# An attention block with a gated feed-forward part on one Trainium2 core: pools of the output projection and of the feed-forward part laid at two ends of SBUF, and the first three feed-forward weights split beside the last row blocks of the projection

## Chip, cores and metric

The kernel runs on one core of one Trainium2 chip. The metric is the device time of one execution in microseconds (us). A change of 0.2% (5.65 us) is about what a measurement of this kernel can tell from no change.

## The reference

One layer of a pre-normalised residual block, for an input x of 2048 rows by 1024 columns in float32. Cut to what matters:

```
u = rms_norm(h, norm1_w);  p = u @ w_in
y_A = differential attention (4 heads);  y_B = stick-breaking attention (8 heads)
h = h + concat(y_A, y_B) @ w_out
u2 = rms_norm(h, norm2_w)
h = h + (silu(u2 @ w_gate) * (u2 @ w_up)) @ w_down      # w_gate, w_up: 1024 x 2816; w_down: 2816 x 1024
```

## The kernel before

Every float32 operand is split into two float16 parts (a rounded value `hi` and a rest `lo`, under a power-of-two scale), and each product is three float16 matmuls. The order of the instructions on each engine is fixed beforehand by a scheduler that follows the text, priorities and its own timeline; each engine and the DMA queue of SyncE (SP) then works its list strictly in order. Nearly all transfers are issued on SP's queue.

**First part.** Eight groups of heads are projected and attended (`proj`, `diff_attn`, `sb_attn`). While the last group is attended, `out_proj` (line 744) begins: for each of 16 row blocks t it loads the mixed heads (`mt`) and the block of x (`xf`), makes four sums of 24 matmuls of 128x128 by 128x256 in two PSUM banks (tag `pj`, line 758), adds them into `xf` on VectorE (DVE, line 761) and writes `xf` to the DRAM tensor `hd`. For t below 12, `post` (line 773) also normalises the block and `x_ops` (line 226) forms from each pair of blocks seven operands for Strassen-like products, written to `xcd[0]` (rows 0 to 1023) and `xcd[1]` (rows 1024 to 2047). Row blocks 12 to 15 are normalised later, by `build_x`.

**Second part.** The feed-forward width of 2816 is cut into 11 pieces (fg) of 256, and the rows into two halves of 1024: 22 steps. A step has a gate `quad` and an up `quad`, each of seven products of 12 matmuls of 128x128 by 128x512 (line 917) on the seven operands X of the half and one split weight (`wg`, `wu`); after every second step `down` (line 1007, its matmuls in line 1014) follows with `wd` on the two steps' activations. So the first `down` of the kernel stands after the gate products of step 2.

In the first half each weight piece is prepared by `load_ffn` (line 833): a 1 MB load into `fst` (two buffers, line 815), squares on ScalarE (`sq`, line 850) or the maximum (line 185), sums over rows on TensorE (`fsc`, line 858 for wg and wu, line 178 for wd), a short chain of small DVE operations for the scale, then `hi` (lines 211, 213, 215), `lo` (line 216, DVE) and the sums of blocks (line 99). The result, 1.8 MB, is also written to the DRAM tensor `split`, from which the second half reads it. The `fst` buffer is free for the next load when its weight is split, so on SP's list a `split` write and the next `fst` load stand one behind the other, as a pair of 2.8 MB.

`build_x` (line 1063) runs during steps 0 and 1: it loads blocks 12 to 15 from `hd` (`bx`), normalises them and forms their operands. It does so in eight rounds: split into float16 (`b`), a DMA transposition of `b` into one buffer (line 236), and a write of that buffer to `xcd[1]` (line 237). The buffer is single, so a round's transposition waits for the write of the round before. The tile `b16` that holds all this is one of the two buffers of the tag `act`; the activations of step 0 take the other one, and those of step 1 (line 976) wait until the last write has read `b16`.

All of the first part's pools are closed, and the second part's opened over them: the first instruction of the new pools waits until the old ones are done with. The loads of X and of the first weights are held to an order with the `mt` loads by hand (`XO`, `WO`, `after_mt`).

Of the kernel before, what the change touches and what calls it, by code (L numbers as in the profile page):

```python
# [39 lines left out]
XO = (10, 13, 14, 15, 11, 12, 15)  # L40
WO = (10, 14, 15)
# [19 lines left out]
def block(tc, a, out):  # L61
# [3 lines left out]
    with top:  # L65
# [44 lines left out]
        def nm(s):  # L110
            uid[0] += 1
            return f"{s}{uid[0]}"
# [138 lines left out]

        with ExitStack() as ph1:
            sp = ph1.enter_context(tc.tile_pool(name="sp", bufs=2))
            bias = sp.tile([P, 4, 256], F32, name="bias", bufs=1)
            ps = ph1.enter_context(tc.tile_pool(name="ps", bufs=2, space=PSUM))
            zp = ph1.enter_context(tc.tile_pool(name="zp", bufs=1))
            pjs = ExitStack()
            pp = pjs.enter_context(tc.tile_pool(name="pp", bufs=2))
# [22 lines left out]
            def load_w(g, st=None):  # L281
# [6 lines left out]
                pt = ps.tile([P, 512], F32, tag="pj", name=nm("wsc"))  # L288
# [26 lines left out]
            @pri("pm")  # L315
            def proj_tile(G, xt):
                pj = ps.tile([P, 512], F32, tag="pj", name=nm("pj"))
# [81 lines left out]
            @pri("spl")  # L399
            def split_t(src, n, he="ADP", le="DP"):  # L400
                s16 = sp.tile([P, 2048], F16, tag="s16", bufs=SB, name=nm("s16"))
# [286 lines left out]
            mpt = ps.tile([P, 512], F32, tag="pj", name=nm("msc"))  # L688
# [30 lines left out]
            wos, kos, mts, rp2 = [], [], [], []  # L719

            def load_wo(n):
                if n in (0, 3):
                    t16 = pp.tile([P, 2 * KT * 384], F16, tag="w16", bufs=2, name=nm("wo"))
                    hi, lo = t16[:, :2048], t16[:, 2048:4096]
                elif n == 1:
                    t16 = pp.tile([P, KT, 384], F32, tag="wst", bufs=1, name=nm("wo"))[:].rearrange("p k n -> p (k n)").bitcast(F16)
                    hi, lo = t16[:, :2048], t16[:, 2048:4096]
                else:
                    hi, lo = (pp.tile([P, 4, 256], F32, tag="raw", name=nm("wo"))[:].rearrange("p t n -> p (t n)").bitcast(F16) for _ in range(2))
# [4 lines left out]
                sW = weight_scale([st[:, :D] for st in sts], rW[:], pW[:], ps.tile([P, 512], F32, tag="pj", name=nm("osc")), hi[:, :D].bitcast(mybir.dt.bfloat16))  # L734
# [9 lines left out]
            def out_proj():  # L744
                for t in range(NT):
# [3 lines left out]
                    xf = pp.tile([P, 6, 4, 2, 64], F16, tag="st", name=nm("xf"))[:].rearrange("p c t s e -> p (c t s e)").bitcast(F32)[:, :D]  # L749
                    SP.dma_start(xf, x[t * P : (t + 1) * P, :])  # L750
                    for h in range(2):
                        po = ps.tile([P, 512], F32, tag="pj", name=nm("po"))
# [19 lines left out]
            @pri("ox")  # L772
            def post(t, xf):
                if t % 2 == 0:
                    held[:] = [z4(), z4()]
                xn = held[t % 2]
                norm_tile(xf, xn[:, :D], w2)
                for h in range(2):
                    ACT.copy(xn[:, 512 * h : 512 * h + 512], transposed(xn, 512 * h)[:])
                note("D", 1150)  # L780
                note("A", 1000)
                if t % 2 == 1:
                    for _ in x_ops([z[:, :D].rearrange("p (d n) -> p d n", d=2) for z in held], z4()[:, :D].rearrange("p (d n) -> p d n", d=2), t // 8, t % 8 // 2, lambda: (sp.tile([P, 2048], F16, tag="s16", bufs=SB, name=nm("x16"))[:], None)):
                        pass
# [11 lines left out]
            for _ in op:  # L796
                pass
            pjs.close()

        with ExitStack() as ph2:  # L800
            ps2 = ph2.enter_context(tc.tile_pool(name="ps2", bufs=2, space=PSUM))
            fw = ph2.enter_context(tc.tile_pool(name="fw", bufs=2))
            xops = []
            for o in range(7):
                xp = ph2.enter_context(tc.tile_pool(name=f"xp{o}", bufs=1))
                xops.append(xp)
            fp = ph2.enter_context(tc.tile_pool(name="fp", bufs=2))
            hp = ph2.enter_context(tc.tile_pool(name="hp", bufs=1))
            r_2, p_2, r_24 = rp2
            scales = {}  # L810

            def after_mt(d, k):
                tc.add_manual_dep(d.ins, mts[k].ins.name, mybir.DependencyInfo(mybir.DependencyClass.NoSync, mybir.DependencyReason.DATA), reason="issue order")

            def stage(fg, nme):
# [6 lines left out]
                if fg == 0:  # L822
                    after_mt(d, WO["gud".index(nme)])
                return st

            ones = hp.tile([P, P], BF16, name="ones", bufs=1)
# [6 lines left out]
            def load_ffn(half, fg, names, W):  # L833
                eng = "ADP" if fg == 0 else WE
                sc = scales.setdefault(fg, {})
                for nme in names:
                    if half == 1:
                        yield
                        late = nme == "d" and fg == NFG - 1
                        w16 = fw.tile([P, 7, 2, 512], F16, tag="wd" if nme == "d" and not late else "wgu", bufs=2, name=nm("w" + nme))  # L840
# [12 lines left out]
                    w16 = fw.tile([P, 7, 2, 512], F16, tag="wd" if nme == "d" else "wgu", bufs=2, name=nm("w" + nme))  # L853
                    pt = ps2.tile([P, 512], F32, tag="b", bufs=8, name=nm("fsc"))
# [65 lines left out]
            def quad(wv, X, tag, bufs, c11, hook=None):  # L920
                def pst(t):
                    return ps2.tile([P, 512], F32, tag="b", bufs=8, name=nm(t))

# [83 lines left out]
            def down(half, units, hs, last, hook=None):  # L1007
# [8 lines left out]
                def pst():  # L1016
                    return ps2.tile([P, 512], F32, tag="b", bufs=8, name=nm("pd"))

# [6 lines left out]
                for j in range(4):  # L1025
# [9 lines left out]
                    pa = pst()  # L1035
# [3 lines left out]
                    pb = pst()  # L1039
                    prod(pb, 4, 4, j)  # L1040
                    acc(u2[:], pb, u2[:])
                    pc = pst()
# [4 lines left out]
                    pd = pst()  # L1047
# [5 lines left out]
                    pe = pst()  # L1053
# [29 lines left out]

            ticks = build_x()
# [5 lines left out]
            level()  # L1090
            steps = [(h, f) for h in range(2) for f in range(NFG)]
            units = []
            W = {}
            X = None
            hs = None
            for i, (half, fg) in enumerate(steps):
                if fg == 0:
                    if half == 0:
                        load_now(0, 0, "g", W)
                    X = [None] * 7  # L1100
                    for o in (0, 4, 5, 1, 2, 6, 3):
                        X[o] = xops[o].tile([P, 4, 2, 4, P], F16, tag=f"X{o}", name=nm("X"))
                        d = SP.dma_start(X[o][:].rearrange("p t s k n -> p (t s k n)"), xcd[half][o].rearrange("p t n -> p (t n)"))
                        if half == 0:
                            after_mt(d, XO[o])
                    if half == 0:
                        load_now(0, 0, "u", W)
# [22 lines left out]
                def in_down():  # L1130
                    end("g")
                    begin("d", half, fg, "d", W)
# [47 lines left out]
```

## Time and profile before

| | |
|---|---|
| median of 3 runs | 2825.47 us (2822.91 to 2825.56) |
| the profiled execution, its time | 2822.35 us |
| its span, first to last instruction | 2820.6 us |
| TensorE busy / VectorE / ScalarE / GpSimd | 89% / 71% / 48% / 52% |
| mean granted TensorE clock | 0.957 |
| bytes moved by DMA | 555.57 MB, mean 197 GB/s |

A profile names instructions by engine (PE: TensorE matmuls, PEld its weight loads, DVE, ACT, POOL, SPq: issues on SP's queue), line, operation and tiles (out<-in). In a timeline a row is its start, its length, what it is and, in brackets, how long the engine had been idle before it and what it had waited for. In the table by stretches a number with (x) is an engine's busy time with its count of instructions; behind them stand the granted clock, the DMA engines' busy share and GB/s. DMA rows give the size and the median time from issue to landing.

### The profile page before, as it was taken

The numbers are of one execution on the slowest core, as the hardware profiler recorded it, in microseconds if no ns is written. First come the engines' busy times: TensorE is split into PE (matmuls) and PEld (weight loads), VectorE is DVE, ScalarE is ACT, GpSimd is POOL, SyncE is SP. The second block draws the span as 40 slices with busy tenths as digits, with TensorE's granted clock in tenths as the row PEclk, the third lists the DMA queues.
The fourth block names the chain that finished last, engine by engine and source line by source line (L and its number), as shares of the span: only waits on it lengthen the run. The fifth ranks groups of instructions, "written<-read, shape, count | busy, mean of one in ns | idle before, by whom it ended". The sixth has DMA issues, their size and how long they took to land.

```text
span 2820.6 us, 45459 instructions
## 1 busy us (share of the span) xinstructions
PE 2505.3 (89%) x17052; PEld 1410.6 (50%) x17052; DVE 2003.0 (71%) x3780; ACT 1358.3 (48%) x2534; POOL 1452.7 (52%) x1011
## 2 busy tenths in 40 slices
PE   7998888988888776789887798989989999999997
PEld 4565555555555443467773344444444444444443
DVE  6898879787989999876729677777785643434435
ACT  4665656467777888655615434444342212111111
POOL 3567767664545545546626456556564332322323
PEclk9999999999999798999998899999999999999998
DMA  7788888789999898987978855656656744645634
GB/s 235 193 164 177 161 175 169 175 173 202 216 196 203 158 189 150 194 182 198 217 257 272 256 193 181 220 198 211 217 203 250 302 164 165 224 143 186 219 128 164
DMA packets 663724, 555.57 MB, mean 197 GB/s; under 512 B 521216, under 2 KB 588800, under 8 KB 653264
## 3 DMA queue, kind: packets, MB, share of 16 engines
q1 hardware_dynamic: 661680, 550.59, 72.0%
q8 instruction: 133, 2.18, 0.3%
q0 software_dynamic: 512, 1.36, 0.2%
q10 hardware_dynamic: 1312, 0.72, 0.1%
q14 instruction: 87, 0.71, 0.1%
HBM read 265.27 MB, written 151.52 MB: 148 GB/s over the span
## 4 chain that ended last, share of the span: by engine, by line
PE 36%; DVE 11%; DMA 9%; issue 5%; POOL 4%; ACT 4%; SPq 1%; DVEq 0%; POOLq 0%; ACTq 0%
PE pd L1014 14%; PE pm L917 8%; PE pa L917 6%; PE pd L917 5%; DVE z L559 4%; DMA aT<-s 2%; POOL s L99 2%; DVE wd L216 1%; DMA fst<-in_w_up_dram 1%; DMA fst<-in_w_down_dram 1%; PE po L758 1%; DVE z L560 1%; PE pj L322 1%; DMA xcd<-b 1%; DMA b<-b 1%
## 5 line engine op out<-in xcount | busy, mean ns | idle before, releaser
L99 POOL TENSOR_TENSOR s<-z,s 128x1024 f16<-128x1024 f32 (+7 forms) x288 | 474.7, 1657 | 330.9 <-ACT s L90 301.1
L322 PE MATMUL pj<-w,xt 128*128 128x384 f16 x3072 | 571.6, 334 | 25.4 <-DMA xt<-xs 9.0
L1014 PE MATMUL pd<-wd,act 128*128 128x512 f16 x1848 | 412.4, 383 | 16.3 <-ACT act L976 8.7
L322 PEld LDWEIGHTS <-xt 128*128 128x128 f16 x3072 | 300.3, 100 | 235.1 <-issue 37.5
L450 PE MATMUL sc<-kT,qT 128*128 128x512 f16 (+3 forms) x1280 | 347.0, 361 | 76.1 <-DVE z L560 27.6
L559 DVE TENSOR_TENSOR_SCAN z<-z,sc 128x512 f32<-128x512 f32 (+3 forms) x320 | 355.4, 1113 | 74.0 <-ACT sc L557 71.3
L460 PE MATMUL yp<-v,aT 128*128 128x64 f16 (+1 forms) x4896 | 282.1, 208 | 78.3 <-DMA aT<-s 77.7
L460 PEld LDWEIGHTS <-aT 128*128 128x128 f16 x4896 | 245.3, 102 | 169.4 <-DMA aT<-s 107.0
L99 POOL TENSOR_TENSOR act<-cg,act 128x512 f16<-128x512 f32 x118 | 165.3, 1410 | 284.7 <-ACT act L976 284.7
L99 POOL TENSOR_TENSOR hs<-hs,cu 128x512 f32<-128x512 f32 x138 | 178.5, 1301 | 249.4 <-DVE cu L1023 103.3
L917 PEld LDWEIGHTS <-wg 128*128 128x128 f16 x1848 | 184.9, 100 | 243.6 <-issue 33.8
L1014 PEld LDWEIGHTS <-act 128*128 128x128 f16 x1848 | 181.7, 98 | 239.2 <-issue 14.6
L917 PEld LDWEIGHTS <-wu 128*128 128x128 f16 x1848 | 181.7, 98 | 216.0 <-issue 2.9
L1023 DVE SCALAR_TENSOR_TENSOR hs<-pd,c,hs 128x512 f32<-128x512 f32 x192 | 143.0, 748 | 167.1 <-PE pd L1014 161.0
L90 ACT CAST s<-z 128x384 f16<-128x384 f32 (+7 forms) x216 | 170.2, 789 | 143.2 <-DMA aT<-s 62.0
L99 POOL TENSOR_TENSOR fst<-fst 128x512 f32<-128x512 f32 x94 | 173.0, 1840 | 122.2 <-DVE wg L216 37.6
L556 ACT ACTIVATE z<-sc,c 128x512 f32<-128x512 f32 (+3 forms) x320 | 203.3, 635 | 20.0 <-PE sc L450 10.0
L560 DVE TENSOR_TENSOR z<-sc,z 128x512 f32<-128x512 f32 (+3 forms) x320 | 193.1, 605 | 7.7
L758 PE MATMUL po<-wo,mt 128*128 128x256 f16 x1536 | 184.1, 278 | 14.8 <-DVE xf L761 14.3
L557 ACT ACTIVATE sc<-sc,c 128x512 f32<-128x512 f32 (+3 forms) x320 | 195.5, 611 | 0.0
L976 ACT CAST act<-cg 128x512 f16<-128x512 f32 x132 | 80.4, 616 | 235.3 <-DVE cg L982 187.9
L917 PE MATMUL pm<-X,wg 128*128 128x512 f16 x792 | 178.3, 379 | 2.6 <-POOL wg L215 2.6
(228 smaller groups left out, 4034.7 us busy)
## 6 DMA issues: line engine op xcount, KB each, us to landing
xt<-xs SPq DMA_DIRECT2D x112, 512.0 KB, 4.4
hs<-hd SPq DMA_DIRECT2D x96, 512.0 KB, 4.3
hd<-hs SPq DMA_DIRECT2D x80, 512.0 KB, 2.9
split<-wg SPq DMA_DIRECT2D x11, 1792.0 KB, 6.9
split<-wu SPq DMA_DIRECT2D x11, 1792.0 KB, 6.7
split<-wd SPq DMA_DIRECT2D x11, 1792.0 KB, 6.8
wg<-split SPq DMA_DIRECT2D x11, 1792.0 KB, 7.3
wd<-split SPq DMA_DIRECT2D x11, 1792.0 KB, 8.3
```

The lines of the kernel that those rows point to most:

```text
L90: ACT.copy(dst, src)
L99: (DVE if e == "D" else POOL).tensor_tensor(dst, a_, b_, op)
L322: PE.matmul(pj[:, :384], lhsT=xv[:, xi, kt, :], rhs=G["w"][:, wi, kt, :], start=n == 0, stop=n == 23)
L450: PE.matmul(sc[:, : 128 * w].rearrange("p (t n) -> p t n", n=P), lhsT=G["q"][i // 4][:, 2 - 2 * o + m, i % 4, :], rhs=G["k"][q][:, m, 0:w, ...
L460: PE.matmul(yp[:, y0 : y0 + wd], lhsT=aT[:, a_, :], rhs=v[:, v_ : v_ + wd], start=start and j == 0 and q == 0, stop=stop and j == nb - 1 a ...
L556: ACT.activation(om[:, lo:hi], sc[:, :w], AF.Sigmoid, scale=G["nkz"][:])
L557: ACT.activation(sc[:, :w], sc[:, :w], AF.Sigmoid, scale=G["kz"][:])
L559: DVE.tensor_tensor_scan(ov, ov, sc[:, :w], om[:, hi : hi + 1], op0=ALU.mult, op1=ALU.bypass)
L560: DVE.tensor_tensor(be[:, lo:hi], sc[:, :w], om[:, lo + 1 : hi + 1], ALU.mult)
L758: PE.matmul(po[:, sl], lhsT=mt[:, kt, P * xi : P * xi + P], rhs=wos[2 * h + n][wi][:, kt, :], start=q == 0, stop=q == 23)
L917: PE.matmul(ps_[:].rearrange("p (t n) -> p t n", n=P), lhsT=wv[:, wo, wi, 128 * kt : 128 * kt + 128], rhs=X[xo][:, :, xi, kt, :], start=st ...
L1014: PE.matmul(po[:], lhsT=act[:, ao, xi, 128 * j : 128 * j + 128], rhs=W["d"][:, wo, wi, :], start=start and u == 0 and q == 0, stop=u == nu ...
```

## The change

The pool `pp` of the projections and the output projection goes to the right end of SBUF, and so do the two `pj` banks of PSUM. The second part's pools are opened at the left end while `out_proj` still has blocks 12 to 15 to do; each of their tiles waits only for the old tiles that lie under it. The float16 buffers `s16` and the bias get a pool of their own, and `wd` one of its own (`fd`). `xf` of blocks 12, 13 and 14 lies in spare room of the output weights' tiles and is loaded far earlier. PSUM tiles of the second part come from the six banks of `ps2` and, every fourth one, from the two `pj` banks; before, from eight in `ps2`. The text now splits wg, wu and wd of piece 0 between the last row blocks, where before wg and wu came behind them and wd in step 0; the hand-made order of loads is gone. The line numbers of the new kernel differ: 758 has become 765, 917 929, 1014 1023, 99 98.

```
+XL = (0, 4, 5, 1, 2, 6, 3)
...
+        psj = top.enter_context(tc.tile_pool(name="psj", bufs=2, space=PSUM, side="right"))
+        pjs = ExitStack()
+        pp = pjs.enter_context(tc.tile_pool(name="pp", bufs=2, side="right"))
...
+            s16p = ph1.enter_context(tc.tile_pool(name="s16p", bufs=1))
...
+                    spare[13 if n == 0 else 14] = t16[:, 4096:6144]
...
+                    spare[12] = t16[:, 4096:6144]
...
+                    if t in spare:
+                        xf = spare[t].bitcast(F32)
...
-            for _ in op:
-                pass
-            pjs.close()
+            while outs < 12:
+                next(op)
+                outs += 1
...
-            ps2 = ph2.enter_context(tc.tile_pool(name="ps2", bufs=2, space=PSUM))
-            fw = ph2.enter_context(tc.tile_pool(name="fw", bufs=2))
+            ps2 = ph2.enter_context(tc.tile_pool(name="ps2", bufs=2, space=PSUM, reuse_waits="tile"))
+            fw = ph2.enter_context(tc.tile_pool(name="fw", bufs=2, reuse_waits="tile"))
...
+            open_x(XL[:6])
+            fd = ph2.enter_context(tc.tile_pool(name="fd", bufs=2, reuse_waits="tile"))
...
+            def pst(t):
+                pst_n[0] += 1
+                if pst_n[0] % 4:
+                    return ps2.tile([P, 512], F32, tag="b", bufs=6, name=nm(t))
+                return psj.tile([P, 512], F32, tag="pj", name=nm(t))
...
+            level()
+            load_now(0, 0, "g", W)
+            load_x(0, XL[:3])
+            next(op)
+            next(op)
+            load_now(0, 0, "u", W)
+            load_x(0, XL[3:6])
+            next(op)
+            next(op)
+            for _ in op:
+                pass
+            load_now(0, 0, "d", W)
+            pjs.close()
+            open_x(XL[6:])
+            load_x(0, XL[6:])
+            fp = ph2.enter_context(tc.tile_pool(name="fp", bufs=2, reuse_waits="tile"))
+            hp = ph2.enter_context(tc.tile_pool(name="hp", bufs=1, reuse_waits="tile"))
...
                 def in_down():
                     end("g")
-                    begin("d", half, fg, "d", W)
+                    if i > 0:
+                        begin("d", half, fg, "d", W)
```

How it moves the lists, at three places. First TensorE's list in the output projection; `po` are its sums, `mt_19514` is block 13 (row blocks before stand in the same order). The change has:

```order
L765 MATMUL po_19462<-wo_16201,mt_19408 128x256
L765 LDWEIGHTS mt_19514
L765 MATMUL po_19517<-wo_14903,mt_19514 128x256
...
L870 LDWEIGHTS ones
L870 MATMUL fsc_19368<-sq_19365,ones 128x256
...
L765 MATMUL po_19568<-wo_15737,mt_19514 128x256
```

The row sums of the first gate weight (`fsc_19368`) have come into block 13; those of the up weight stand in the same way ahead of block 14. Before, both stood behind the last row block, where this piece has its end:

```order
L758 MATMUL po_19697<-wo_16195,mt_19642 128x256
L858 LDWEIGHTS ones
L858 MATMUL fsc_19796<-sq_19793,ones 128x256
...
L858 MATMUL fsc_19852<-sq_19849,ones 128x256
...
L917 LDWEIGHTS wg_19795
L917 MATMUL pa_19882<-X_19830,wg_19795 128x512
```

Second, SP's list around the start of `build_x`, before; `bx` are its loads, `b` its transpositions, `xcd_83<-b` its writes:

```order
L1077 DMA bx_19949<-hd 128x1024
L899 DMA split<-wg_19795 128x7168
L821 DMA fst_19940<-in_w_gate_dram 128x8x256
L236 DMA_TRANSPOSE b_19953<-b_19953 128x16x128
L899 DMA split<-wu_19851 128x7168
L819 DMA fst_20052<-in_w_down_dram 128x2x1024
L237 DMA xcd_83<-b_19953 128x2x1024
```

And with the change:

```order
L1083 DMA bx_19992<-hd 128x1024
L911 DMA split<-wd_19885 128x7168
L835 DMA fst_20155<-in_w_up_dram 128x8x256
L235 DMA_TRANSPOSE b_19996<-b_19996 128x16x128
L236 DMA xcd_83<-b_19996 128x2x1024
L235 DMA_TRANSPOSE b_19996<-b_19996 128x16x128
```

The first transposition and its write have no weight between them any more; gate and up of piece 0 are ahead of all this, and the write of `wd` of piece 0 with the load of the next up weight stands ahead of the first transposition. Over the eight rounds, between the first transposition and the last write, SP's list before has seven such pairs (writes of wu0, wg1, wd0, wu1, wg2, wd1, wu2, the digit being the piece), and with the change five (wg1, wu1, wg2, wd1, wu2).

Third, VectorE's list at the same point; `m` and `c` are the small operations of a scale. The change has:

```order
L215 SCALAR_TENSOR_TENSOR wd_19885<-fst_19877,c_19881,wd_19885 128x2x512
L871 TENSOR_REDUCE m_20062<-fsc_20061 128x1
L942 TENSOR_TENSOR cg_19938<-pm_19940,cg_19938 128x512
L195 TENSOR_SCALAR m_20062<-m_20062 128x1
L946 TENSOR_TENSOR cg_19967<-pm_19954,cg_19938 128x512
L170 TENSOR_SCALAR c_19986<-m_20062 128x1
L171 TENSOR_SCALAR c_19986<-c_19986 128x1
L172 TENSOR_SCALAR c_19985<-c_19986 128x1
L130 TENSOR_SCALAR c_20091<-c_19986,c_14895 128x1
L199 TENSOR_SCALAR c_19987<-c_19985 128x1
L130 TENSOR_SCALAR c_20092<-c_19985,c_14894 128x1
L1072 TENSOR_SCALAR bx_19990<-bx_19990,c_14896 128x1024
```

Before, the first operation of `build_x` (line 1066) stood in the middle of the up weight's split:

```order
L859 TENSOR_REDUCE m_19853<-fsc_19852 128x1
L99 TENSOR_TENSOR fst_19788<-fst_19788 128x4x128
L196 TENSOR_SCALAR m_19853<-m_19853 128x1
L171 TENSOR_SCALAR c_19847<-m_19853 128x1
L172 TENSOR_SCALAR c_19847<-c_19847 128x1
L1066 TENSOR_SCALAR bx_19947<-bx_19947,c_14890 128x1024
```

It has moved behind the whole split of `wd` of piece 0 and behind the row sums of the gate weight of piece 1.

More of the change, by code (lines that the diff above doesn't have):

```diff
@@ L287, in load_w @@
                 rW, pW = c1(), c1()
-                pt = ps.tile([P, 512], F32, tag="pj", name=nm("wsc"))
+                pt = psj.tile([P, 512], F32, tag="pj", name=nm("wsc"))
                 if first:
@@ L316, in proj_tile @@
             def proj_tile(G, xt):
-                pj = ps.tile([P, 512], F32, tag="pj", name=nm("pj"))
+                pj = psj.tile([P, 512], F32, tag="pj", name=nm("pj"))
                 xv = xt[:].rearrange("p (s k n) -> p s k n", s=2, k=KT)
@@ L400, in split_t @@
             def split_t(src, n, he="ADP", le="DP"):
[L401 removed]
+                s16 = s16p.tile([P, 2048], F16, tag="s16", bufs=SB, name=nm("s16"))
                 to16(s16[:, :n], src, n, he)
@@ L687, in block @@
             absmax(mm0[:], mgain[:])
-            mpt = ps.tile([P, 512], F32, tag="pj", name=nm("msc"))
+            mpt = psj.tile([P, 512], F32, tag="pj", name=nm("msc"))
             across(mm1[:], mpt, [mm0[:]])
@@ L782, in post @@
                 if t % 2 == 1:
-                    for _ in x_ops([z[:, :D].rearrange("p (d n) -> p d n", d=2) for z in held], z4()[:, :D].rearrange("p (d n) -> p d n", d=2), t // 8, t % 8 // 2, lambda: (sp.tile([P, 2048], F16, tag="s16", bufs=SB, name=nm("x16"))[:], None)):
+                    for _ in x_ops([z[:, :D].rearrange("p (d n) -> p d n", d=2) for z in held], z4()[:, :D].rearrange("p (d n) -> p d n", d=2), t // 8, t % 8 // 2, lambda: (s16p.tile([P, 2048], F16, tag="s16", bufs=SB, name=nm("x16"))[:], None)):
                         pass
@@ L839, in load_ffn @@
                         late = nme == "d" and fg == NFG - 1
-                        w16 = fw.tile([P, 7, 2, 512], F16, tag="wd" if nme == "d" and not late else "wgu", bufs=2, name=nm("w" + nme))
+                        w16 = (fd if nme == "d" and not late else fw).tile([P, 7, 2, 512], F16, tag="wd" if nme == "d" and not late else "wgu", bufs=2, name=nm("w" + nme))
                         SP.dma_start(w16[:].rearrange("p o s n -> p (o s n)"), split[fg, "gud".index(nme)])
@@ L1082, in build_x, with load_x @@
                     yield from x_ops([d2(z) for z in (xa, xb)], d2(xt), 1, j, bufs, "AP", "DP")
+            W = {}
+            X = [None] * 7
+            def load_x(half, os):
+                for o in os:
+                    X[o] = xops[o].tile([P, 4, 2, 4, P], F16, tag=f"X{o}", name=nm("X"))
+                    SP.dma_start(X[o][:].rearrange("p t s k n -> p (t s k n)"), xcd[half][o].rearrange("p t n -> p (t n)"))
+            level()
[15 more added lines that the diff above has]
+            hp = ph2.enter_context(tc.tile_pool(name="hp", bufs=1, reuse_waits="tile"))
             ticks = build_x()
@@ L1088, in tick @@
                     next(ticks, None)
-            level()
             steps = [(h, f) for h in range(2) for f in range(NFG)]
             units = []
-            W = {}
-            X = None
             hs = None
             for i, (half, fg) in enumerate(steps):
[L1097 to L1107, printed above, removed]
+                if i == NFG:
+                    load_x(1, XL)
                 due = len(units) == 2 or (fg == 0 and units)
```

50 lines of the change are left out of this document (19 added, 31 removed).

## Prediction

> **What bounds the kernel now.** I read the page, then the table by stretches around the end of the output projection, then TensorE's timeline for its waits, then the chain of waits for who ended last. The stretches, TensorE's busy time first, the clock, DMA share and GB/s last:
>
> ```profile
> core 0: us, PE busy (x) PEld busy (x) DVE busy (x) ACT busy (x) POOL busy (x), PEclk, DMA share, GB/s
> 1440.00:1476.60 36.60, 27.81 (x235) 23.54 (x232) 4.82 (x11) 1.91 (x1) 1.27 (x1) 0.91 0.76 280
> 1476.60:1486.10 9.50, 3.48 (x16) 2.33 (x17) 4.06 (x13) 3.56 (x3) 0.00 (x0) 0.70 0.70 263
> 1486.10:1540.70 54.60, 41.19 (x181) 18.31 (x179) 49.85 (x64) 26.23 (x31) 39.55 (x23) 0.91 0.80 258
> 1540.70:1600.00 59.30, 46.23 (x199) 21.42 (x199) 52.11 (x74) 29.52 (x35) 38.06 (x22) 0.85 0.86 265
> 1600.00:1624.00 24.00, 19.95 (x87) 8.27 (x86) 8.74 (x8) 9.60 (x13) 8.49 (x6) 0.92 0.70 231
> ```
>
> TensorE idles 8.8 us in the last row blocks, 6.0 before the first product, then 13.4, 13.1 and 4.1 until the first `down`: 45.4 us in all, of which the change could at most take all. VectorE has 4.8 us of work in the first stretch and over 100 in the next three. The waits by name:
>
> ```profile
> 1428.71 21.12 PE L758 MATMUL po<-wo,mt 128*128 128x256 f16 x192
> 1455.82 12.58 PE L758 MATMUL po<-wo,mt 128*128 128x256 f16 x96 [5.99 <-DVE xf L761]
> 1471.12 5.40 PE L758 MATMUL po<-wo,mt 128*128 128x256 f16 x48 [2.72 <-DVE xf L761]
> 1480.57 1.86 PE L858 MATMUL fsc<-sq,ones 128*128 128x256 bf16 x8 [4.05 <-DVE ones L827]
> 1486.14 3.25 PE L917 MATMUL pa<-X,wg 128*128 128x512 f16 x12
> 1513.81 1.35 PE L858 MATMUL fsc<-sq,ones 128*128 128x256 bf16 x8
> 1517.58 5.34 PE L917 MATMUL pm<-X,wu 128*128 128x512 f16 x24
> 1540.69 1.86 PE L858 MATMUL fsc<-sq,ones 128*128 128x256 bf16 x8 [7.19 <-ACT sq L850]
> 1596.67 1.87 PE L858 MATMUL fsc<-sq,ones 128*128 128x256 bf16 x8 [7.10 <-ACT sq L850]
> 1621.29 10.93 PE L1014 MATMUL pd<-wd,act 128*128 128x512 f16 x36 [3.95 <-ACT act L976]
> ```
>
> Row blocks 14 and 15 wait for their `xf`; the projection ends at 1476.5; the first product starts at 1486.1; then TensorE waits for weights, and at 1621.29 for the activations of step 1. That last wait is the one that counts, since everything after it follows from where the first `down` starts. What ScalarE waited for there:
>
> ```profile
> 1620.62 1.66 ACT L976 CAST act<-cg 128x512 f16<-128x512 f32 x3 [11.14 <-DMA xcd<-b]
> ```
>
> It had been idle 11.1 us, for the last write of `build_x`, whose tile holds the buffer. So two lines of work race to 1621: the weights with the products, and the eight rounds of `build_x`. The rounds came last. They are a chain of transfers; from the chain of waits:
>
> ```profile
> 1503.85 5.17 DMA b<-b
> 1509.08 12.17 DMA xcd<-b
> 1521.27 4.22 DMA b<-b
> ...
> 1609.40 7.64 DMA b<-b
> 1617.13 3.47 DMA xcd<-b
> ```
>
> From the first transposition to the end of the last write it takes 1620.6 - 1503.85 = 116.8 us, eight rounds of 14.6.
>
> **The change part by part.** *Weights beside the row blocks.* SP's issues that matter here, the squares on ScalarE, and the time from issue to landing of the first gate weight:
>
> ```profile
> 1424.65 0.42 SPq L763 DMA_DIRECT2D hd<-xf  x1
> ...
> 1480.65 0.43 SPq L1065 DMA_DIRECT2D bx<-in_norm_w_dram  x1
> ...
> 1508.11 0.33 SPq L899 DMA_DIRECT2D split<-wu  x1
> 1508.47 0.43 SPq L819 DMA_DIRECT2D fst<-in_w_down_dram  x1
> 1509.08 0.83 SPq L237 DMA_DIRECT2D xcd<-b  x1
> ```
>
> ```profile
> 1458.12 1.91 ACT L850 ACTIVATE sq<-fst 128x2048 bf16<-128x2048 f32 x1 [22.19 <-DMA fst<-in_w_gate_dram]
> ```
>
> ```profile
> fst<-in_w_gate_dram SPq DMA_DIRECT2D x1, 1024.0 KB, 14.2
> ```
>
> In the new order the load stands right behind the `hd` write of block 11, which went out at 1424.65. So it is issued at about 1425.1, lands at 1439.3 and is squared by 1441.2. TensorE's `fsc` for it stands, counted from the last product of the attention, which both orders have at the same place, at the 108th matmul of the row of 192 that starts at 1428.71: 108 x 0.11 = 11.9, or 1440.6. It waits 0.6 us. The two `xf` waits (8.7 us) go, as three of the four blocks have their `xf` long before. Behind the first `fsc` are 276 matmuls x 0.11 = 30.4 us and two `fsc` of 1.35 each (the row of 1513.81): the projection ends at 1474.3, some 2.5 us earlier than now, and the first product follows it at once instead of at 1486.1. VectorE's and GpSimd's part of the splits lies beside the blocks, where VectorE has 4.8 us of work in 36.6; if that cover were short, TensorE would wait for a PSUM bank behind line 761's additions.
>
> *wd of piece 0* now stands before the first product's VectorE work, and the first operations of `build_x` stand behind it on VectorE and ScalarE. The splits of wd0 took no part in the rounds' start before. That costs the rounds something at their start only if `bx` has landed by then; it lands late:
>
> ```profile
> bx<-hd SPq DMA_DIRECT2D x4, 512.0 KB, 10.5
> ```
>
> I take 0, and for the upper end of the range 2 us, one of the operations of 1.91 above. *PSUM tiles* still turn over in a ring of eight: nothing. *Early `xf` loads* put three transfers of 0.5 MB into the attention, and the lists there are slightly reordered; no row gives that a sign, and I take 0.
>
> *The rounds.* Their start moves with the end of the projection: `bx` goes out 2.5 us earlier. What is between them changes more. In SP's list before, seven pairs of a `split` write and an `fst` load stand ahead of one of the sixteen transfers of the chain, in the new one five. The price of a pair: the first write, with the pair of 1508.11 ahead of it, took 12.17 us; without one, the nearest rows are these, the first from the end of the projection, the others from the rounds:
>
> ```profile
> xcd<-x SPq DMA_DIRECT2D x2, 512.0 KB, 5.2
> ```
>
> ```profile
> xcd<-b SPq DMA_DIRECT2D x6, 512.0 KB, 10.2
> ...
> xcd<-b SPq DMA_DIRECT2D x2, 256.0 KB, 2.9
> b<-b SPq DMA_TRANSPOSE x8, 4.9
> ```
>
> So 12.17 - 5.2 = 7.0 us a pair, at most 12.17 - 2.9 = 9.3, and at least nothing, if the time goes with all that is in flight rather than with what is ahead. I take 7.0, since the 5.2 is a transfer of the same size: 2 x 7.0 = 14.0 us. With 2.5 of the start that is **16.5 us**. If transfers in flight shared the bandwidth instead, the pair of wd0 just ahead of the first round would still be in the way, one pair would be saved, and the gain would be 9.5 us; the 12.17 with the pair 0.6 to 1 us ahead agrees with either. The Trainium skill (DMA: Bandwidth & Descriptors, Queues, rings and completion order) says that on each DMA engine the transfers of one issuing engine are consumed in ring order; by that rule what is ahead delays a transfer and what is behind does not, both pairs count in full, and the sum is the 16.5.
>
> The TensorE side is faster than that. From 1474 to the `fsc` of the up weight of piece 2, which in the new order stands at the end of the gate products of step 2, are 32.8 products of 5.34 / 2 = 2.67 us, 87.6 us, and three `fsc` of up to 1.87: 1474.3 + 87.6 + 5.6 = 1567.5. So the weights are early, and the 45.4 us of idle time turn into one wait at the activations of step 1: TensorE will stand there from about 1575 to 1604.
>
> The sum: first `down` at 1621.3 - 16.5 = 1604.8, and from there the same work in the same order. The profiled execution took 2822.35 us, 3.1 below the median of the runs. 2822.35 - 16.5 = 2805.9, and against the median 2825.47 - 16.5 = **2809 us**. All differences below are against the median.
>
> **The rivals.** *The rounds do not hold it back* (0.15). If each round shrinks as TensorE and VectorE run ahead, the next gate is the split of the up weight of piece 2, which stands ahead of the last transposition on SP's list:
>
> ```profile
> 1609.02 0.33 SPq L899 DMA_DIRECT2D split<-wu  x1
> ```
>
> It came 10.5 us after its `fsc` (end 1598.5). So 1567.5 + 1.9 + 10.5 = 1579.9, then 7.64 + 0.1 + 3.47 for the last round: 1591.1, a gain of 29.5 us, or 2796. For it speaks that the splits run well ahead of the rounds; against it, that the rounds' own transfers alone are 16 x 5 = 80 us.
>
> *Nothing is gained* (0.12). The rounds start no earlier, as wd0 stands ahead of them on three engines, and the pairs cost as much in flight as ahead. Then the waits only move: within 0.2%, 2820 to 2831. For it: the chain is the same eight rounds, and the projection ends only 2.5 us earlier.
>
> *Slower: the first `fsc` blocks the projection* (0.11). TensorE, ScalarE and VectorE work in order: if the gate weight lands late, the `fsc` in block 13 holds three blocks behind it, ScalarE's squares hold the casts of `x_ops` for blocks 10 and 11, and VectorE's block sums on `fst` hold line 761. DMA is full there:
>
> ```profile
> 1450.00:1460.00 10.00, 4.18 (x21) 2.91 (x21) 0.88 (x2) 1.88 (x1) 1.27 (x1) 0.66 1.04 400
> ```
>
> From 1425 to 1474 some 17.9 MB would now be wanted: six X and four `fst` of 1 MB, two `split` of 1.8, and 4.3 of smaller ones. At 400 GB/s that is 44.8 us of 49. If the two weights came 10 us late each, with the loads of `bx` queued behind, the projection would end at about 1494, 17 later than now, and the rounds with it; with one pair of 7 saved, which is what a shared queue would give, that makes +10, or 2836. It decides from where the projection ends past 1490, since the 14 us of the pairs are then used up. Against it: the 14.2 us of the load above were already spent behind three X of 1 MB:
>
> ```profile
> 1438.96 2.71 SPq L1103 DMA_DIRECT2D X<-xcd  x3
> ...
> 1443.78 0.38 SPq L821 DMA_DIRECT2D fst<-in_w_gate_dram  x1
> ```
>
> **How the numbers follow.** My forecast, the rounds with a gain of 6 to 26 us, has 0.62. Faster by over 0.2% (5.65 us, about what a measurement of this kernel can tell from no change): 0.62 + 0.15 = 0.77; within 0.2%: 0.12; slower: 0.11. For the range, the low end is 2791, just past the rival of 29.5 us (0.05 left out), the high end 2828, which takes in most of no change and leaves out the slower case and a little (0.13).
>
> **What would show it.** Right: `fsc` rows inside the rows of line 765; the last of these at about 1474 and the first product right behind; first transposition at 1500 to 1504, the first write under 7 us; TensorE's one long wait of some 25 us for the activations of step 1, ended by a write `xcd<-b` near 1604. Wrong: if that wait is short and the first `down` stands near 1591 (rounds not in the way), or if the last row block ends past 1480. A difference that is there before 1400 would come from the attention and be no part of my reasons.

## The result and the profile after

The changed kernel takes 2776.67 us (median of 4 runs, 2774.53 to 2778.39) beside 2824.27 us for the kernel before on the same chip (4 runs): a ratio of 0.9831, 95% interval 0.9814 to 0.9848, 47.6 us faster. The profiled execution has a span of 2775.3 us, 45.3 less than before. The forecast was 16.5 us and the low end of its range 2791: the direction was right, the size was not.

The table by stretches for the changed kernel: the last row blocks, the products up to the point where TensorE stalls (two rows), that stall, the first `down` from there to its first write to `hd`, and the stretch from that write to the first `hd` write of the fifth `down`, eight steps later (called steps 3 to 10 below).

```profile
core 0: us, PE busy (x) PEld busy (x) DVE busy (x) ACT busy (x) POOL busy (x), PEclk, DMA share, GB/s
1434.50:1469.70 35.20, 30.94 (x280) 27.13 (x279) 22.77 (x39) 11.30 (x11) 19.02 (x13) 1.00 1.02 404
1469.70:1526.00 56.30, 54.09 (x260) 25.29 (x258) 42.20 (x63) 27.57 (x34) 35.52 (x22) 1.00 0.71 234
1526.00:1572.20 46.20, 42.99 (x198) 19.88 (x197) 40.20 (x61) 27.56 (x32) 28.39 (x19) 0.96 0.89 274
1572.20:1596.83 24.63, 0.02 (x1) 0.00 (x1) 2.65 (x3) 3.62 (x4) 4.80 (x4) 0.57 0.80 256
1596.83:1611.40 14.57, 14.47 (x61) 5.95 (x62) 12.15 (x15) 7.17 (x12) 9.57 (x7) 0.90 0.00 1
1611.40:2092.30 480.90, 458.26 (x2153) 213.13 (x2152) 370.42 (x528) 209.52 (x249) 291.54 (x192) 0.99 0.61 212
```

VectorE now has 22.8 us of work beside the row blocks, where it had 4.8. TensorE's idle time of the second stage has become one stall, as forecast. Its timeline at the places that the prediction named:

```profile
1433.67 1.04 PE L870 MATMUL fsc<-sq,ones 128*128 128x256 bf16 x8
1442.95 1.04 PE L870 MATMUL fsc<-sq,ones 128*128 128x256 bf16 x8
...
1452.67 2.78 PE L765 MATMUL po<-wo,mt 128*128 128x256 f16 x24 [1.76 <-DVE wo L768]
1456.59 13.26 PE L765 MATMUL po<-wo,mt 128*128 128x256 f16 x120 [1.13 <-DVE wo L768]
1469.68 2.75 PE L929 MATMUL pa<-X,wg 128*128 128x512 f16 x12
...
1565.58 1.03 PE L870 MATMUL fsc<-sq,ones 128*128 128x256 bf16 x8 [0.62 <-ACT sq L862]
...
1569.47 2.75 PE L1023 MATMUL pd<-wd,act 128*128 128x512 f16 x12
1596.83 8.22 PE L1023 MATMUL pd<-wd,act 128*128 128x512 f16 x30 [24.61 <-ACT act L985]
```

The first product stands right behind the projection; the waits in the row blocks are now for VectorE's additions (line 768), 1 to 2 us each; the last `fsc` before the stall is at 1565.58 (forecast 1567.5); the stall ends at 1596.83, which was to be 1604.8. What ended it, from the chain of waits:

```profile
1545.99 4.25 DMA b<-b
1550.26 5.25 DMA xcd<-b
1555.53 11.12 DMA b<-b
1566.71 10.34 DMA xcd<-b
1577.07 4.29 DMA b<-b
1581.37 2.77 DMA xcd<-b
1584.16 9.59 DMA b<-b
1593.81 2.28 DMA xcd<-b
1596.16 2.19 ACT act L985 x4
```

The rounds of `build_x` still come last, and all eight run in 1596.16 - 1494.04 = 102.1 us instead of 116.8. SyncE's row of the first transposition:

```profile
1494.04 2.73 SPq L235 DMA_TRANSPOSE b<-b  x1
```

So the first waited `down` comes 1621.29 - 1596.83 = 24.5 us earlier: 9.8 from the start of the rounds (1503.85 to 1494.04) and 14.7 from their length. The other 20.8 us of the 45.3 come later. The same steps 3 to 10 in the kernel before take 501.90 us where the changed kernel takes 480.90:

```profile
1635.90:2137.80 501.90, 466.51 (x2154) 215.71 (x2153) 372.23 (x528) 211.28 (x250) 297.62 (x191) 0.97 0.59 207
2137.80:2820.60 682.80, 665.10 (x3065) 300.32 (x3062) 309.00 (x417) 119.97 (x185) 220.38 (x173) 0.99 0.54 195
```

Behind them nothing differs (682.8 us here, 2775.3 - 2092.3 = 683.0 with the change). What TensorE waited for in steps 3 to 10, before (us in total, times, longest):

```profile
PE fsc L858 <- ACT sq L850: 28.1, 8, 6.7
PE fsc L178 <- ACT sq L185: 5.4, 2, 3.7
PE pd L917 <- DVE cg L947: 1.7, 2, 0.9
PE pa L917 <- ACT cg L930: 0.2, 1, 0.2
```

And with the change:

```profile
PE pd L1023 <- DVE cu L963: 6.4, 2, 3.6
PE fsc L177 <- ACT sq L184: 5.8, 3, 3.2
PE pd L929 <- DVE cg L956: 4.6, 3, 2.8
PE fsc L870 <- ACT sq L862: 3.9, 2, 2.0
PE pm L929 <- ACT cg L974: 1.7, 1, 1.7
```

The waits of the row sums of gate and up weights have shrunk from 28.1 to 3.9 us. Part of it comes back as waits for VectorE (6.4 and 4.6), and TensorE's own time falls by 8.3 us (466.51 to 458.26) at a granted clock of 0.99 instead of 0.97.

Why that is shows in the scheduler's lists. In the second part 493 PSUM tiles are first written by TensorE. Before, with one tag of eight banks, all 493 stand in the order of the text; with two tags, of six banks and two, each tag keeps the text's order but 97 tiles stand elsewhere. So before, an `fsc` that waits for its load holds every product behind it in the text; with the change a product whose tile has the other tag may stand ahead of it. Of the 33 row-sum tiles among the 493, 14 are overtaken by a product that comes later in the text, and 36 products are overtaken by other products; before, none is.

### The profile page after: what moved, and what is told of

Its sections match the earlier page's. It is cut to its first block, busy times and chain, and to the rows that moved or that the text cites. A ratio compares the mean times of both kernels' runs of the same rounds, so it can differ in the third digit from the quotient of the medians.

```text
span 2775.3 us, 45405 instructions
## 1 busy us (share of the span) xinstructions
PE 2494.1 (90%) x17052; PEld 1409.4 (51%) x17052; DVE 1984.4 (72%) x3776; ACT 1358.5 (49%) x2535; POOL 1442.9 (52%) x1014
## 4 chain that ended last, share of the span: by engine, by line
PE 35%; DVE 7%; DMA 6%; POOL 3%; issue 3%; ACT 2%; SPq 0%; DVEq 0%; POOLq 0%; ACTq 0%
PE pd L1023 14%; PE pm L929 8%; PE pd L929 6%; PE pa L929 6%; DVE wd L215 2%; PE po L765 2%; DMA aT<-s 1%; DMA fst<-in_w_down_dram 1%; DMA b<-b 1%; DVE wu L215 1%; POOL s L98 1%; DMA xcd<-b 1%; DVE cg L991 1%; POOL fst L98 1%; DVE cg L98 1%
## 5 line engine op out<-in xcount | busy, mean ns | idle before, releaser
L324 PE MATMUL pj<-w,xt 128*128 128x384 f16 x3072 | 579.9, 338 | 26.0 <-DVE st L334 10.2
L929 PEld LDWEIGHTS <-wu 128*128 128x128 f16 x1848 | 181.3, 98 | 223.6 <-issue 10.6
L765 PE MATMUL po<-wo,mt 128*128 128x256 f16 x1536 | 181.9, 277 | 10.6 <-DVE xf L768 6.3
L929 PE MATMUL pm<-X,wu 128*128 128x512 f16 x792 | 180.3, 380 | 4.8 <-ACT cg L974 4.6
```

The source lines that it names most:

```text
L765: PE.matmul(po[:, sl], lhsT=mt[:, kt, P * xi : P * xi + P], rhs=wos[2 * h + n][wi][:, kt, :], start=q == 0, stop=q == 23)
L929: PE.matmul(ps_[:].rearrange("p (t n) -> p t n", n=P), lhsT=wv[:, wo, wi, 128 * kt : 128 * kt + 128], rhs=X[xo][:, :, xi, kt, :], start=st ...
```

## The experiments

Theory: three parts of the change bring the gain (the early `xf`, the fewer pairs between the rounds, the two tags), and the ring of PSUM tiles, which the prediction put at nothing, is one of them. Rival, the prediction's own: the ring costs nothing, and what was gained behind the first `down` comes from weights that are early. Each run stands beside runs of the kernel before, whose median was 2822.92, 2824.47 and 2821.64 us in the three sets. The changed kernel's 2776.67 is from another set, and as these medians differ by 2.8, a difference to it is good to some 3 us. "Steps 3 to 10" is the time between the first `hd` writes of the first and of the fifth `down` in the run's own profile; "rounds" is from the first transposition to the end of the last write.

**The ring, alone and taken away.** The edit on the kernel before (its three places that take a tile of the eight now call `pst`):

```
+            def pst(t):
+                pst_n[0] += 1
+                if pst_n[0] % 4:
+                    return ps2.tile([P, 512], F32, tag="b", bufs=6, name=nm(t))
+                return ps2.tile([P, 512], F32, tag="pj", bufs=2, name=nm(t))
```

> The kernel before with one part of the change alone: its PSUM tiles of the second part come from two tags, six banks and two (every fourth tile), instead of one tag of eight banks. In the scheduler's list of before, all 493 PSUM tiles of the second part are first written in text order; with two tags 91 stand elsewhere, in the changed kernel 97. Theory of the prediction (the ring costs nothing, the gain comes from the rounds of build_x and from early weights): 2824, no difference. Theory of the tags (a product whose tile has the other tag may pass a row sum that waits, so TensorE's waits in steps 3 to 10 shrink from 35 us to some 23, and half the gain is the ring's): two steps of the first half take 121 us in place of 126, from step 3 on some 20 us in all, so 2800 to 2806.

Measured: 2799.39 us, ratio 0.9915 (0.9900 to 0.9931), 23.5 faster. Steps 3 to 10 take 484.1 us instead of 501.9; the rest of the gain lies ahead of them, where the first `hd` write comes at 1629.63 instead of 1635.88. The converse, on the changed kernel:

```
+            p6 = ExitStack()
+            ps2 = [p6.enter_context(tc.tile_pool(name="ps6", bufs=2, space=PSUM, reuse_waits="tile")), 6]
...
-                pst_n[0] += 1
-                if pst_n[0] % 4:
-                    return ps2.tile([P, 512], F32, tag="b", bufs=6, name=nm(t))
-                return psj.tile([P, 512], F32, tag="pj", name=nm(t))
+                return ps2[0].tile([P, 512], F32, tag="b", bufs=ps2[1], name=nm(t))
...
             pjs.close()
+            p6.close()
+            ps2[:] = [ph2.enter_context(tc.tile_pool(name="ps2", bufs=2, space=PSUM, reuse_waits="tile")), 8]
```

> The changed kernel with one tag of eight PSUM banks from the first product on (the pool of six and the two banks of the projection are closed before it). Weights beside the row blocks, early xf, and the pools at two ends stay. Theory of the prediction: 2777, no difference to the changed kernel. Theory of the tags: the first waited down stands near 1597 as in the changed kernel (within 5 us), and the 20 us behind it are lost again: 2797, two steps of the first half taking 126 us.

Measured: 2793.49 us, ratio 0.9896 (0.9880 to 0.9912): 16.8 us of the gain are lost. The first waited `down` stands at 1594.56, as early as in the changed kernel, but steps 3 to 10 take 500.4 us. Its waits there are like those of the kernel before:

```profile
PE fsc L868 <- ACT sq L860: 33.6, 8, 6.0
PE fsc L177 <- ACT sq L184: 2.6, 2, 1.7
```

Early weights with one tag gain nothing in steps 3 to 10; two tags with late weights gain 17.8 of the 21 us. The prediction's "nothing" for the ring has fallen.

**What may pass what.** The changed kernel with row sums alone on the small tag (`if t != "fsc"` in place of the count of four): products stand in text order among themselves, but a row sum holds none of them.

> The changed kernel with the row sums fsc alone on the tag of two PSUM banks, and all products on the tag of six. A waiting row sum now never holds the tile of a product, but the products stand in text order among themselves. Theory of the tags (what was lost in steps 3 to 10 was products behind a waiting row sum): two steps of the first half take 121 us or less, in the changed kernel 121, total 2770 to 2777. If instead a product passing a product is what helps, the 126 us of before come back: 2797. Theory of the prediction: no difference.

Measured: 2795.18 us, ratio 0.9901 (0.9881 to 0.9921). The total is close to the 2797 of the second theory, but by chance: the loss stands ahead of step 3, not in steps 3 to 10. 53 matmuls of products (12.7 us) have moved in among the last row blocks, the first at 1443.17, and TensorE waits 11.7 us there instead of 4.3; the first transposition comes at 1514.04, 20.0 us late, and the rounds end near 1614 instead of 1596. Steps 3 to 10 take 478.5 us, the least of these runs, and the waits for gate and up row sums there are down to one:

```profile
PE pd L928 <- DVE cg L955: 12.2, 7, 3.6
PE pa L928 <- ACT cg L938: 5.1, 3, 2.7
PE pa L928 <- ACT cu L938: 2.2, 2, 1.4
PE fsc L869 <- ACT sq L861: 1.8, 1, 1.8
```

In this run's list 14 row sums are overtaken by products again, and no product by a product. So in steps 3 to 10 it was the row sum holding the products that cost some 20 us, not products holding products. Four tags of two banks (`tag=f"b{pst_n[0] % 4}"`, two banks each, in place of the six) add nothing by themselves:

> The changed kernel with four tags of two PSUM banks each instead of six and two: 112 of 493 tiles are first written out of text order, in the changed kernel 97. Theory of the tags: two steps of the first half take 121 us or a few us less, total 2765 to 2778. Theory of the prediction: 2777.

Measured: 2774.36 us (2769.99 to 2780.58), ratio 0.9826 (0.9805 to 0.9847), not to be told from the changed kernel.

**Early xf.** On the changed kernel, `if t in spare:` became `if False:`.

> The changed kernel with the xf of blocks 12, 13 and 14 in the old buffers, loaded as late as before. If the xf waits of before (5.99 and 2.72 us) are gone because of the early loads, the projection ends 6 to 9 us later than 1469.7, the rounds start as much later and the total is 2783 to 2786. If the early weights alone filled those waits, 2777 to 2779.

Measured: 2794.48 us, ratio 0.9899 (0.9882 to 0.9916), 17.8 us more than the changed kernel, twice what was expected. TensorE's row of the wait, and SyncE's loads of `xf`:

```profile
1464.57 12.52 PE L765 MATMUL po<-wo,mt 128*128 128x256 f16 x96 [8.22 <-DVE xf L768]
...
1486.87 5.40 PE L765 MATMUL po<-wo,mt 128*128 128x256 f16 x48
```

```profile
1447.61 0.33 SPq L757 DMA_DIRECT2D xf<-in_x_dram  x1
1450.79 0.32 SPq L770 DMA_DIRECT2D hd<-xf  x1
1465.07 4.54 SPq L757 DMA_DIRECT2D xf<-in_x_dram  x1
```

Blocks 14 and 15 wait for their `xf`, the one of block 15 being issued only at 1465.07; gate products fill much of the time, so the wait itself looks small, but the projection ends at 1492.3 and the first transposition stands at 1512.59, 18.5 us late. The rounds take what they took in the changed kernel (101), and the total moves by about as much as their start: 17.8. The rounds start even later here than in the kernel before (1503.85): the loads of these two `xf` stand among the transfers of the early weights and take 15.5 and 14.4 us, where they took 12.9 and 3.3. Then the same part alone, on the kernel before:

```
+                    spare[13 if n == 0 else 14] = t16[:, 4096:6144]
...
+                    spare[12] = t16[:, 4096:6144]
...
+                    xf = spare[t].bitcast(F32) if t in spare else pp.tile([P, 6, 4, 2, 64], F16, tag="st", name=nm("xf"))...
```

> The kernel before with one part of the change alone: the xf of blocks 12, 13 and 14 lie in spare room of the output weights' tiles and are loaded far earlier. SyncE's list of the rounds stays that of before, with seven pairs. Theory that the start of the rounds carries through to the end one for one: the two xf waits of 5.99 and 2.72 us go, the first transposition stands at about 1495, the total at 2814 to 2817. Theory that the gate weights and their row sums set the first product in before, so that the waits only move: 2822 to 2825.

Measured: 2805.77 us, ratio 0.9938 (0.9923 to 0.9953), 15.9 us faster. The projection ends at 1465.6, 10.9 us earlier than before, and the first transposition stands at 1492.70, 11.2 us earlier, although the weights come behind the row blocks as they did. The first waited `down` comes 11.7 us earlier (1609.61), so the start carries through to there; another 4.0 us come in steps 3 to 10 (497.9), within what the kernels with one tag differ by. So the early `xf` alone are enough for a start as early as the changed kernel's, and without them it is lost.

**wd of piece 0.** The changed kernel without `load_now(0, 0, "d", W)` and without the condition `i > 0`.

> The changed kernel with the down weight of piece 0 prepared in step 0 again, as before; gate and up of piece 0 stay beside the row blocks. On SyncE's list six pairs of a split write and an fst load stand between the first transposition and the last write, in the changed kernel five. Theory of the pairs (7 us each ahead of the chain of rounds): the first transposition 3 us earlier, as the pair of wd0 no longer stands ahead of it, the last write 4 us later, 2781. Theory that the first rounds wait for VectorE and ScalarE: these have the split of wd0 between the rounds again, some 9 us of VectorE, and the last write lands 5 to 9 us later: 2782 to 2786. Theory that the start of the rounds is what counts: 2774.

Measured: 2796.67 us, ratio 0.9904 (0.9887 to 0.9920), 20.0 us more than the changed kernel; all three numbers were too low. The first transposition stands at 1497.03, 3.0 us later, and the last write lands near 1615.5, so the rounds take 118.5 us, 16.4 more. How they are made up shows in the times from issue to landing of the sixteen transfers, in order (T transposition, W write; from the DMA view at each issue):

```
before               T  5.2  4.2 11.3  4.5  4.2  4.3  6.7  7.6
                     W 12.2  2.8 10.7  2.3 10.3  8.1 10.1  3.5   sum 108.0 of 116.8
changed kernel       T  4.3  4.3  4.2  9.4  4.2 11.1  4.3  9.6
                     W  2.7 12.4  2.8  2.9  5.3 10.3  2.8  2.3   sum  92.9 of 102.1
wd0 in step 0        T  4.9  4.4 12.7  7.6  5.4 12.4  4.3  3.1
                     W  2.7 10.7  5.0  3.7 11.2  2.7 10.6  2.3   sum 103.7 of 118.5
```

A transfer with nothing ahead of it takes 4.2 (T) or 2.8 us (W), in the fourth and the eighth round, where the write has half the size, 3.0 and 2.3; one just behind a pair mostly takes 9 to 12. Two pairs fewer than before make 108.0 - 92.9 = 15.1 us less, 7.5 a pair, where the prediction had 7.0. Sixteen transfers with nothing ahead would take some 52.6 us by these numbers (6 x 7.0 + 2 x 5.3), which leaves 7.9 a pair for the seven of before, 8.1 for the five of the changed kernel and 8.5 for the six of this run. One pair more with `wd` in step 0 makes 10.8 us; the other 5.6 are time between the transfers (14.8 us instead of 9.2), in which they may wait for engines that have the split to do as well; that was not traced to an engine.

**Is it the place on the queue?** The pairs of pieces 1 and 2 were issued by ScalarE (`ACT.dma_start` for `fg in (1, 2)`, loads and writes), the rounds stayed with SyncE.

> The changed kernel with the split writes and fst loads of pieces 1 and 2 issued on ScalarE's queue instead of SyncE's; nothing stands ahead of the sixteen transfers of the rounds on SyncE's list any more except a gate load of piece 3. In the changed kernel the sixteen took 92.9 us from issue to landing, five of them, behind a pair, 9.4 to 12.4, the others mostly 2.3 to 4.3. Theory of the order on the queue (a transfer waits for what is ahead of it on its own queue): the five come down to 3 to 4 us, the rounds from 102 to some 70 us, the first waited down stands at about 1572 where the weights end it, and the total is 2752 to 2758. Theory of sharing (what is in flight delays it, whatever queue it is on): the five stay near 10 us and the total within 5 us of 2777. ScalarE waits for the splits itself now, which may cost either theory some us.

Measured: 2783.66 us, ratio 0.9854 (0.9833 to 0.9875), 7 us more than the changed kernel: the first transposition came 7.5 us later, the rounds took some 100 us as before. A pair on ScalarE's queue, then the next transposition on SyncE's, 2.3 us behind it, and its time to landing:

```profile
1519.61 0.35 ACTq L912 DMA_DIRECT2D split<-wg  x1
1519.99 0.46 ACTq L836 DMA_DIRECT2D fst<-in_w_gate_dram  x1
```

```profile
1522.24 8.77 SPq L235 DMA_TRANSPOSE b<-b  x1
```

```profile
b<-b SPq DMA_TRANSPOSE x1, 11.8
```

It still took 11.8 us, and three more transfers behind a pair on ScalarE's queue were slow: the one at 1562.27 took 10.9, and the two short writes at 1543.46 and 1594.04 took 6.6 and 7.7 where 2.3 is usual. The transposition at 1536.83, issued 1.2 us ahead of the next pair, took 3.1, as long as an undisturbed one of its round. What counts is what was issued earlier, on whichever queue; theory "order on the queue" is out, and so is "in flight at all". The rule of the Trainium skill (DMA: Bandwidth & Descriptors, Queues, rings and completion order) that the prediction set beside its 16.5 speaks of the transfers of one issuing engine; here the pairs that one engine issued delayed the transfers of another about as much.

**The rounds as the line that ends last.** The changed kernel with `for j in (2,)` in `build_x`, and blocks 8 and 9 written twice:

> The changed kernel with build_x done for blocks 12 and 13 only: four rounds instead of eight. The operands of blocks 14 and 15 are left out; their places in xcd are filled with those of blocks 8 and 9, written a second time during the attention. Theory that the rounds alone hold the first waited down: TensorE's wait of 24.6 us goes, it stands at about 1572, and the total is 2752 to 2757. Theory that the weights are right behind the rounds (wait comes back as one for a row sum): a gain of less than 10, 2767 or more.

Measured: 2765.75 us, ratio 0.9795 (0.9778 to 0.9812), 10.9 us less than the changed kernel. The wait for activations of step 1 is gone, but the first `down` comes at 1586.13 instead of 1569.47: between 1500 and 1586 TensorE now waits 14.9 us for weights, gate sums and a row sum. So half the rounds gain 11 us, not the 24.6 of the stall; other waits, for weights among them, are right behind, and neither theory had the number. It is no clean price of four rounds, since the lists moved as well: the first transposition comes at 1511.40, 17.4 us later than in the changed kernel.

**Three slots for the rounds**, so that a transposition does not wait for the write before it:

```
-                    n[0] ^= 1
-                    return b16[:, 2048 * n[0] : 2048 * n[0] + 2048], b16[:, 4096:6144]
+                    s, d = 2 * n[0] % 3, (2 * n[0] + 1) % 3
+                    n[0] += 1
+                    return tuple(b16[:, 2048 * k : 2048 * k + 2048] for k in (s, d))
```

> The changed kernel with the three slots of b16 taken in turn, so that a round's transposition does not wait for the write of the round before, only the next cast but one does. Theory that the rounds hold the first waited down as a chain of transposition and write: the writes leave the chain, the last write lands 10 to 25 us before 1596, and the total comes down to what four rounds instead of eight gave, 2766 (2763 to 2770). Theory that the split weights' transfers ahead of each transposition set the pace, or that SyncE's list, where the writes stand ahead of the next transposition, keeps the old order: 2772 to 2777.

Measured: 2785.64 us, ratio 0.9865 (0.9846 to 0.9884): 9 us slower than the changed kernel, which no theory had. The rounds take 110 us and their sixteen transfers 113.0: with write and transposition now side by side behind a pair, nine of them take over 6 us instead of five. On the kernel before:

> The kernel before with the three slots of b16 taken in turn, the same edit. Theory that the rounds were the line that ended last in before too, with the weights some 6 us behind: the wait for the activations of step 1 goes and the total is 2817 to 2820. Theory that the weights, with their waits for row sums at 1540.69 and 1596.67, held it as much: 2822 to 2825.

Measured: 2815.64 us (12 runs, 2806.21 to 2821.98), ratio 0.9975 (0.9962 to 0.9987): a gain of 6.0, the size that the first theory had, though hardly more than a measurement can tell. Its one profile ran longer than that median (a span of 2820.2), so the place is not shown. Both edits together, three slots and four tags, on the changed kernel:

> The changed kernel with both the three slots taken in turn and four tags of two PSUM banks. If the slots free the first waited down and the tags cost nothing: 2762 to 2768, below both kernels. If either does nothing: 2770 to 2777.

Measured: 2760.26 us (2757.90 to 2763.20), ratio 0.9777 (0.9761 to 0.9793): faster than both kernels, 16.4 us below the changed one. Rounds 90 us, the stall at the first `down` 14.3 us, steps 3 to 10 479.7:

```profile
1584.33 10.43 PE L1023 MATMUL pd<-wd,act 128*128 128x512 f16 x36 [14.25 <-ACT act L985]
```

Why the slots gain on the changed kernel only together with the tags was not taken apart. The lists of the two differ in which transfers stand behind a pair.

**What stays open.** Taken away one at a time, the two tags, the early `xf` and the early `wd` cost 16.8, 17.8 and 20.0 us, more in sum than the whole gain of 47.6, so the parts do not simply add. No run takes away the early gate and up weights of piece 0, or the pools at two ends, by themselves.

## Why the prediction was right and wrong

*What bounds the kernel* was right as far as it went: the rounds of `build_x` end last before the first `down`, the last `fsc` ahead of it runs from 1565.58 to 1566.6 (1567.5 said), and the idle time becomes one stall of about 25 us (24.6). Part of the 1567.5 was luck: the projection ended 4.6 us earlier than said, and the products behind it took some 4 us longer. And "they are a chain of transfers" was too simple for the kernel before. Among the rows that the prediction's view leaves out, the chain of waits runs through a weight:

```profile
1583.39 11.23 DMA fst<-in_w_up_dram
...
1594.71 1.92 ACT sq L850
...
1596.67 1.88 PE fsc L858 x8
...
1609.02 0.33 SPq L899
```

Behind this split write SyncE issues the last transposition, at 1609.40; the write of the round before had landed at 1607.8. So weights and rounds were level within some 2 us there, and the gain at the first `down` needed both to come earlier.

*"Two pairs of 7.0 us, 14.0"* held: the rounds got 14.7 us shorter, their transfers 15.1. The 7.0 was luck in part. It stands on one write behind a pair (12.17) and a write of 5.2 from the end of the projection, while a write of the same size in the rounds takes 2.8 with nothing ahead; the difference, 9.4, is what that one write paid, and the average over all pairs is lower. The reason given with it, the order on SyncE's queue, was too narrow.

*"The projection ends at 1474.3, 2.5 us earlier"* failed in the working. Its own difference is 2.2 (1476.5 - 1474.3), a small slip. The 108 matmuls to the first `fsc` were to be counted from the last product of the attention, but were counted from the row at 1428.71, which begins 51 matmuls later: 51 x 0.11 = 5.6 us too late for the first `fsc` (1433.67, not 1440.6). Waits of 4.3 us for VectorE, which the prediction had named as the price if the cover were short, took some back: the projection ended at 1469.7. That is 6.8 us earlier than before, and the first two `bx` went out 5.3 us earlier. Besides, they landed in 6.9 us instead of 10.6; before, two X loads stood 1.3 us ahead of them on SyncE's list, with the change one stands 5.1 us ahead, but that this is the reason was not tested. So the term for the start, 2.5, measured 9.8; the runs show that it hangs on the early `xf`.

*"PSUM tiles still turn over in a ring of eight: nothing"* is the step that failed outright, and with it "from there the same work in the same order": put at 0, it measured 17.8 us in steps 3 to 10 alone on the kernel before, and 19.5 when taken away from the changed kernel (500.4 instead of 480.9). It is true that each bank comes round after eight tiles. But a tag is also an order: its tiles are first written in the order of the text. Two tags let the products pass a waiting row sum. Steps 3 to 10 take 478.5 to 484.1 us in the ten profiles with two or more tags, and 497.9 to 504.1 in the four with one. The prediction asked what the ring makes wait, and not what it lets the scheduler reorder; its orders were of the stretch around the edit only, while the lists differ all through the first half.

*The sum*: 9.8 + 14.7 = 24.5 at the first `down` (16.5 said), and 20.8 behind it (0 said).

*The rivals.* "The rounds do not hold it back", 29.5 us, did not come; with half the rounds the weights do hold, and only 11 us are gained. "The first `fsc` blocks the projection" did not come: the load was squared by 1433.1, before TensorE needed it. "Nothing is gained" did not come either.

## What to carry to other kernels

With a scheduler like this one, a tag of buffers is an order as well as a number of buffers: with one tag, an instruction that waits for data holds all later ones that need a buffer of the same tag, and a second tag for the kind that waits can be worth more than the moves that were planned. Compare the order of the instructions over the whole program, not only around the edit. Where a chain of small transfers ends last, count how many of them are issued shortly behind a large one, on any queue.

## What the runs showed of the hardware

A small transfer issued just behind 2.8 MB mostly took 9 to 12 us instead of 2.3 to 4.3, whether the large ones were issued on its own queue (five of sixteen in the changed kernel) or 2.3 us earlier on another engine's (11.8 us); issued 1.2 us ahead of them it took 3.1. And where TensorE's waits got shorter, its own time got shorter as well: in steps 3 to 10 TensorE's idle time fell by 12.8 us (501.90 - 466.51 = 35.4 to 480.90 - 458.26 = 22.6), its busy time for the same matmuls by another 8.3, with the granted clock at 0.99 instead of 0.97. The clock is 0.97 in all four profiles with one tag and 0.99 in all ten with two or more.
